# Final states of a state-space mixer as fp32r products in three terms

## The chip, the cores and the metric

The kernel runs on one core of a Trainium2 chip. The metric is the device time of one execution in microseconds (us); of several runs the median counts. The engines are called TensorE (PE), VectorE (DVE), ScalarE (ACT), GpSimd (POOL) and SyncE (SP). Each works through its own instructions in order. SP and POOL issue the transfers (DMAs) that this document speaks of.

## The reference, cut to what matters

One layer of a hybrid encoder works on 256 prompt tokens and 32 sample tokens with the same weights. A projection feeds a pooling mixer and a Mamba-2 mixer (SSD) with 32 heads of 64 features and a state of 128. Their outputs go through w_out, a norm and a residual; a feed-forward part (up projection, short convolution, gate, down projection) follows. The change concerns the final state of each head, which is an output beside the token outputs. In one line for a token group, with the tokens' l, the head's feature p and the state index n:

```
h_last[p, n] = sum_l  B[l, n] * decay[l] * dt[l] * x[l, p]   (+ elast * h0[p, n] for the sample)
```

For the prompt the sum runs over 256 tokens and the old state is zero; for the sample it runs over 32 tokens. B is shared by the 16 heads of a group; decay is the decay from token l to the last token.

## The kernel before, in words

The tokens lie on the free axis: 288 columns, 256 of the prompt and 32 of the sample. Features lie on the 128 partitions. All large products are fp32r products in three terms: a value is split into a high part (an fp32r copy by ACT) and a low part (the difference, by DVE), and PE adds high x high, high x low and low x high (`mm3`, L134 to L137). Weights come in by SP (`fetch_w`, L111), four raw buffers deep, and are split in pieces of 1024 columns (`split_w`, L117) into four buffers each for high and low.

`project` (L139) runs one group of 256 output features: per stage of its `ksplit` it fetches the weights, calls a hook (`before`) for the next stage, splits, multiplies, and at the end calls `done` for each accumulator. The instruction order on each engine comes from a scheduler that simulates the program; `keep_in_program_order` pins an instruction to its place on its engine, `issue_after` and `high_priority` steer it.

The work around the change, in order:
- The decay factors (L401 to L416): `dec` is decay times dt on 32 partitions (heads); PE transposes it into `tokd`, token rows of 128 x 32 per block of tokens. The sample's block is the last 128 tokens, with zeros in `tokd` (a memset on POOL) ahead of the 32 sample rows.
- B and x go through DRAM (`b_d`, `xs_d`) to become token rows. `btok` (L586, loaded by SP at L684 and L685) holds B with tokens on partitions: two prompt blocks and the sample's.
- `mix` holds the mixer's outputs as split pairs: 8 tiles of the pooling mixer (`mixp`) and 16 tiles of the SSD mixer (`mixs`, in the 16 slots of `apool`).
- The w_out groups (L740): group pairs 0 and 1 together, then 2 to 7 one by one, each over stages of k 8 to 15 (`mixs` 0 to 7), 16 to 23 (`mixs` 8 to 15) and 0 to 7 (`mixp`). `mix_out` (L668) squares each result into `msum` (ACT, then an addition on POOL) and stores it scaled by the norm's gain (`mg`, list `x1`). The last two squares go to `msq`.
- The states are four parts j of 512 columns (8 heads). `state_in` (L688) loads x rows and old state through POOL's queue, two buffers deep, and scales both on DVE. `state_p` (L706) multiplies two fp32 128x512 products for the prompt, copies the result (ACT) and stores it. `state_s` (L716) multiplies one fp32 product for the sample, copies it (ACT) and adds the old state. Parts 0 and 1 stand behind groups 2 and 3, with that addition on POOL. Parts 3 and 2 are loaded behind groups 4 and 5, and their products are pinned behind the last group and behind the products that finish `p_m` (the mean square, L737 and L758); their additions come on DVE in the line of the up projection (L804).
- The seam: `root(rm, p_m)` is a square root on ACT and a reciprocal on DVE (L235). `residual(t)` (L780) is a product and a sum on DVE; `in_line` (L773) keeps DVE's order. For each of 16 tiles k, ACT makes the high part of `hn` (L791), DVE the low part, ACT a square for the next norm, and PE multiplies seven accumulators (L815 to L820).
- The PSUM pool `acc_ps` has five banks, used in turn; `aux_ps` has three. `bpool` has 20 slots.

Of the kernel before, what the change touches and what calls it, by code (L numbers as in the profile page):

```python
# [8 lines left out]
F32 = mybir.dt.float32  # L9
F32R = mybir.dt.float32r  # L10
AF = mybir.ActivationFunctionType
ALU = mybir.AluOpType
# [4 lines left out]
P = 128  # L17
TC = {"schedule_with_timeline_sim": True}
D_MODEL = 2048
NP_ = 256  # L20
NS = 32
NT = NP_ + NS
# [3 lines left out]
HEADS = 32  # L26
D_FF = 5632
EPS = 1e-6
KD = D_MODEL // P
# [14 lines left out]
def body(  # L44
# [25 lines left out]
    act, dve, pool, pe, sp = nc.scalar, nc.vector, nc.gpsimd, nc.tensor, nc.sync  # L70
# [97 lines left out]
    def blocks_out(d, t, src, pool_):  # L168
# [17 lines left out]
        out=tri, in_=tri, pattern=[[1, P]], compare_op=ALU.is_ge, fill=0.0, base=0, channel_multiplier=-1  # L186
# [30 lines left out]
    start = ExitStack()  # L217
# [199 lines left out]

    bc = []
    for i in range(4):
# [166 lines left out]
    btok = op_.tile([P, 2, 3, P], F32, name="btok")  # L586
# [76 lines left out]
    wov = w_out  # L663
# [15 lines left out]
        x1.append(o)  # L679


    for gi in range(2):
        c = slice(gi * P, (gi + 1) * P)
        sp.dma_start(out=btok[:, gi, 0:2, :], in_=b_d[:NP_, c].rearrange("(b p) c -> p b c", p=P))  # L684
        sp.dma_start(out=btok[:, gi, 2, :], in_=b_d[NT - P :, c])  # L685
    stp = []

    def state_in(j):  # L688

        if not stp:  # L690
            poolp.close()
            stp.append(outp.enter_context(tc.tile_pool(name="stp", bufs=1)))
        x = stp[0].tile([P, 3, 512], F32, tag="sx", bufs=2, name="sx")
        h = stp[0].tile([P, 512], F32, tag="sh", bufs=2, name="sh")
        c = slice(512 * j, 512 * j + 512)
        pool.dma_start(out=x[:, 0:2, :], in_=xs_d[:NP_, c].rearrange("(b p) c -> p b c", p=P))
        pool.dma_start(out=x[:, 2, :], in_=xs_d[NT - P :, c])
        pool.dma_start(out=h, in_=state_ssd[:, c])
        x4 = x.rearrange("p b (r q) -> p b r q", r=8)
        w = tokd[:, :, 8 * j : 8 * j + 8].unsqueeze(3).broadcast_to([P, 3, 8, 64])  # L700
        dve.tensor_tensor(x4, x4, w, op=ALU.mult)
        h3 = h.rearrange("p (r q) -> p r q", r=8)
        dve.tensor_tensor(h3, h3, elast[:, 8 * j : 8 * j + 8].unsqueeze(2).broadcast_to([P, 8, 64]), op=ALU.mult)
        return x, h

    def state_p(j, x, h, pin=False):  # L706
        st = acc_ps.tile([P, 512], F32, tag="acc", name="pst")
        for b in range(2):
            ins = pe.matmul(st, btok[:, j // 2, b, :], x[:, b, :], start=b == 0, stop=b == 1)  # L709
            if pin:  # L710
                tc.keep_in_program_order(ins)
        ho = stp[0].tile([P, 512], F32, tag="ho", bufs=2, name="ho")
        act.activation(ho, st, AF.Copy)
        sp.dma_start(out=new_ssd_p[:, 512 * j : 512 * j + 512], in_=ho)

    def state_s(j, x, h, pin=False):  # L716
        st = acc_ps.tile([P, 512], F32, tag="acc", name="psts")
        ins = pe.matmul(st, btok[:, j // 2, 2, :], x[:, 2, :], start=True, stop=True)  # L718
        if pin:
            tc.keep_in_program_order(ins)  # L720
        act.activation(x[:, 2, :], st, AF.Copy)

        def add(eng=pool):
            ins = eng.tensor_tensor(h, h, x[:, 2, :], op=ALU.add)
            sp.dma_start(out=new_ssd_s[:, 512 * j : 512 * j + 512], in_=h)
            return ins

        return add

    late_in = {}  # L730

    def mix_before(g):
        def hook(kb, n):
            if g == 0 and kb == 0:
                pool_group(0)
            if g == 7 and kb == 0:
                pe.matmul(p_m, mean, msum, start=True, stop=False)  # L737
        return hook

    for grp in ((0, 1), (2,), (3,), (4,), (5,), (6,), (7,)):  # L740
        project(
            wov, [(256 * c, 256) for c in grp], mix, [(8, 8), (16, 8), (0, 8)],
            mix_before(grp[0]), lambda m, p_: mix_out(p_),
        )
        if 2 <= grp[0] < 4:
            x_h = state_in(grp[0] - 2)
            state_p(grp[0] - 2, *x_h)
            state_s(grp[0] - 2, *x_h)()
        elif 4 <= grp[0] < 6:
            late_in[grp[0] - 2] = state_in(grp[0] - 2)  # L750
        if grp[0] == 0:
            sp.dma_start(out=xT, in_=x_in)
            act.dma_start(out=new_sconv, in_=sc_stage)
            act.dma_start(out=new_pool, in_=np_stage)


    for i in range(2):
        tc.keep_in_program_order(pe.matmul(p_m, mean, last_sq[i], start=False, stop=i == 1))  # L758
# [14 lines left out]
    def in_line(f, *args, **kw):  # L773
        with ExitStack() as order:
            if line:
                order.enter_context(tc.issue_after(line[-1].ins))
            line.append(f(*args, **kw))
        return line[-1]

    def residual(t):  # L780
        in_line(dve.tensor_tensor, x1[t], x1[t], rm, op=ALU.mult)
        in_line(dve.tensor_tensor, x1[t], x1[t], xT[:, t, :], op=ALU.add)

    residual(0)
    for k in range(KD):
        if k % 2 == 0:
            raw = wpool.tile([P, 2, 896], F32, tag="raw", name="raw")
            with tc.high_priority(offset=ahead[0]):
                sp.dma_start(out=raw, in_=w_up1[:, k : k + 2, :])
        a = atile("hn")  # L790
        hi = act.activation(a[:, 0, :], x1[k], AF.Copy, scale=g_ffn_pre[:, k : k + 1])  # L791
# [369 lines left out]
```

## Time and profile before

| what | us |
|---|---|
| median of three runs (lowest, highest) | 1323.76 (1323.6, 1324.56) |
| the profiled execution | 1324.25 |
| its span (first to last instruction) | 1322.5 |
| PE busy in the span | 1314.3 (99%) |
| DVE busy | 882.4 (67%) |
| ACT busy | 667.3 (50%) |
| POOL busy | 222.4 (17%) |

Times in the rows of the profile are us from the span's start unless marked ns. The chain of work is followed back from the last instruction; each row is a start, a length, an engine and a line. PE's products overlap: the distance of two starts is what one costs, and it is shorter than the duration printed for it. A product in fp32 leaves two records, one in fp32r leaves one. "x4" counts records. In rows of the form "min/median/max" durations are in ns, landings of DMAs in us. The rows of stretches (windows) give the stretch, its length, then busy us of PE, PE's weight loads, DVE, ACT and POOL with their instruction counts, PE's granted clock, the DMA share and GB/s.

### The profile page before, as it was taken

The numbers are of one execution on the slowest core, as the hardware profiler recorded it, in microseconds if no ns is written. First come the engines' busy times: TensorE is split into PE (matmuls) and PEld (weight loads), VectorE is DVE, ScalarE is ACT, GpSimd is POOL, SyncE is SP. The second block draws the span as 40 slices with busy tenths as digits, with TensorE's granted clock in tenths as the row PEclk, the third lists the DMA queues.
The fourth block names the chain that finished last, engine by engine and source line by source line (L and its number), as shares of the span: only waits on it lengthen the run. The fifth ranks groups of instructions, "written<-read, shape, count | busy, mean of one in ns | idle before, by whom it ended". The sixth has DMA issues, their size and how long they took to land.

```text
span 1322.5 us, 25126 instructions
## 1 busy us (share of the span) xinstructions
PE 1314.3 (99%) x10063; PEld 1298.2 (98%) x10063; DVE 882.4 (67%) x1461; ACT 667.3 (50%) x1004; POOL 222.4 (17%) x351
## 2 busy tenths in 40 slices
PE   9999999999999999999999999999999999999998
PEld 9999999999999989999999999999999999999997
DVE  7899997779644379976766643345666666664544
ACT  7558876446443455654444443334444444444443
POOL 7221411211221100211211100001111111101110
PEclk9999999999999999999999999999999999999999
DMA  8668974465666446666454454455544544466653
GB/s 322 204 209 263 291 229 144 159 237 203 226 204 207 149 142 206 199 188 180 166 184 159 152 176 160 163 180 172 179 160 160 178 173 160 163 236 189 201 176 108
DMA packets 104021, 249.82 MB, mean 189 GB/s; under 512 B 63760, under 2 KB 69456, under 8 KB 81504
## 3 DMA queue, kind: packets, MB, share of 16 engines
q1 hardware_dynamic: 101984, 243.11, 56.1%
q0 software_dynamic: 1488, 4.92, 1.1%
q8 instruction: 79, 1.29, 0.4%
q14 instruction: 38, 0.31, 0.1%
q10 hardware_dynamic: 432, 0.19, 0.1%
HBM read 236.23 MB, written 11.95 MB: 188 GB/s over the span
## 4 chain that ended last, share of the span: by engine, by line
PE 99%; DMA 1%; ACT 0%; SPq 0%; issue 0%; DVE 0%
PE acc L135 31%; PE acc L137 31%; PE acc L136 31%; PE acc_x L137 1%; PE acc_x L135 1%; PE py L475 1%; PE acc_x L136 1%; DMA raw<-in_w_first 1%; PE pst L709 1%; PE run_a L1033 0%; PE low L1031 0%; PE run_b L1046 0%; PE py L477 0%; PE psts L718 0%; PE pdt L297 0%; PE py L481 0%
## 5 line engine op out<-in xcount | busy, mean ns | idle before, releaser
L130 DVE TENSOR_TENSOR wlo<-raw,whi 128x1024 fp32r<-128x1024 f32 (+1 forms) x386 | 463.0, 1200 | 340.8 <-ACT whi L129 338.5
L129 ACT ACTIVATE whi<-raw 128x1024 fp32r<-128x1024 f32 (+1 forms) x386 | 400.5, 1038 | 491.1 <-PE acc L136 394.9
L135 PE MATMUL acc<-hn,whi 128*128 128x288 f32 x1360 | 395.6, 295 | 0.0
L136 PE MATMUL acc<-hn,whi 128*128 128x288 f32 x1360 | 394.3, 293 | 0.0
L137 PE MATMUL acc<-hn,wlo 128*128 128x288 f32 x1360 | 393.2, 293 | 0.0
L135 PEld LDWEIGHTS acc<-hn,whi 128*128 128x128 f32 x1360 | 254.3, 188 | 0.5 <-ACT xsum L799 0.2
L136 PEld LDWEIGHTS acc<-hn,whi 128*128 128x128 f32 x1360 | 253.9, 188 | 0.1
L137 PEld LDWEIGHTS acc<-hn,wlo 128*128 128x128 f32 x1360 | 253.7, 188 | 0.0
L135 PE MATMUL acc<-xn,whi 128*128 128x288 f32 x688 | 203.1, 297 | 1.1 <-ACT whi L276 1.1
L136 PE MATMUL acc<-xn,whi 128*128 128x288 f32 x688 | 200.2, 293 | 0.0
L137 PE MATMUL acc<-xn,wlo 128*128 128x288 f32 x688 | 195.0, 295 | 0.0
L135 PE MATMUL acc<-fa,whi 128*128 128x288 f32 x660 | 194.2, 294 | 0.0
L136 PE MATMUL acc<-fa,whi 128*128 128x288 f32 x660 | 193.6, 293 | 0.0
L137 PE MATMUL acc<-fa,wlo 128*128 128x288 f32 x660 | 193.2, 293 | 0.0
L135 PEld LDWEIGHTS acc<-xn,whi 128*128 128x128 f32 x688 | 129.7, 189 | 2.8 <-ACT whi L276 1.4
L136 PEld LDWEIGHTS acc<-xn,whi 128*128 128x128 f32 x688 | 129.5, 188 | 0.2
L137 PEld LDWEIGHTS acc<-xn,wlo 128*128 128x128 f32 x688 | 126.5, 188 | 0.0
L135 PEld LDWEIGHTS acc<-fa,whi 128*128 128x128 f32 x660 | 124.2, 188 | 0.0
L137 PEld LDWEIGHTS acc<-fa,wlo 128*128 128x128 f32 x660 | 123.9, 188 | 0.0
L136 PEld LDWEIGHTS acc<-fa,whi 128*128 128x128 f32 x660 | 123.9, 188 | 0.0
L844 POOL COPY fc_stage<-ebuf 128x4 f32<-128x4 f32 x88 | 28.5, 324 | 526.4 <-DVE ebuf L843 455.5
L850 DVE SCALAR_TENSOR_TENSOR fc<-ebuf,pf,fc 128x290 f32<-128x290 f32 x176 | 90.0, 517 | 2.9 <-ACT fc L848 0.3
(286 smaller groups left out, 1701.6 us busy)
## 6 DMA issues: line engine op xcount, KB each, us to landing
raw<-in_w_up SPq DMA_DIRECT2D x80, 1024.0 KB, 4.8
raw<-in_w_in SPq DMA_DIRECT2D x38, 1024.0 KB, 5.1
raw<-in_w_down SPq DMA_DIRECT2D x32, 1024.0 KB, 4.8
raw<-in_w_out SPq DMA_DIRECT2D x24, 1024.0 KB, 4.8
raw<-in_w_down SPq DMA_DIRECT2D x16, 768.0 KB, 4.4
raw<-in_w_up SPq DMA_DIRECT2D x8, 896.0 KB, 4.5
gb<-g_d SPq DMA_DIRECT2D x8, 832.0 KB, 6.0
raw<-in_w_first SPq DMA_DIRECT2D x7, 768.0 KB, 9.0
```

The lines of the kernel that those rows point to most:

```text
L129: act.activation(hi, raw[:, k : k + n, :], AF.Copy)
L130: dve.tensor_tensor(lo, raw[:, k : k + n, :], hi.bitcast(F32), op=ALU.subtract)
L135: pe.matmul(out, wh, a[:, 0, :], start=start, stop=False)
L136: pe.matmul(out, wh, a[:, 1, :], start=False, stop=False)
L137: pe.matmul(out, wl, a[:, 0, :], start=False, stop=stop)
L475: pe.matmul(y[:, 0:256], xw[:, 0, c], m[:, j, 0:256], start=True, stop=False)
L709: ins = pe.matmul(st, btok[:, j // 2, b, :], x[:, b, :], start=b == 0, stop=b == 1)
L844: pool.tensor_copy(fc_stage[:, :, :, i], e[:, 256:324].rearrange("p (s c) -> p s c", c=34)[:, :, 0:2])
L850: dve.scalar_tensor_tensor(c, e[:, r_ : r_ + 290], pf[:, r_, i : i + 1], c, op0=ALU.mult, op1=ALU.add)
```

## The change

The final states are computed by fp32r products in three terms. B is split once into `bhi` and `blo`; each part's scaled x rows into `hi` and `lo`. A prompt part takes six 128x512 products. For the sample, the 32 token rows are put four times on the partitions (`token_rows`, four DMAs of 32 rows): the quarters hold low or high parts of B and of x such that one 128-row product sums all four terms. `tokd` gets the sample's factors four times as well (`dec_s`).

Part 0 stays behind group 2. Parts 3, 2 and 1 go behind the last group: the three sample products are pinned ahead of the last `p_m` products, the prompt products behind them. The buffers for x, old state and splits become single; part 2's split and all of part 1 live in slots of `apool` (those of the `mixs` tiles, the "tokens") and of `bpool`. Part 1's rows are loaded by POOL when group 7's hook asks for them, into the slots of `mixs` 5 to 7. Old-state additions read PSUM on DVE: those of parts 3 and 2 ahead of the `p_m` products in the program, part 1's in line behind `residual(0)`. In the first tile of the up projection the low part now precedes `residual(1)`. B rows come by POOL's queue, no longer by SP. The last stage of group 7 is split in two.

```diff
@@ decay factors
-    pool.memset(tokd[:, 2, :], 0.0)
+    dec_s = mp.tile([HEADS, 4, NS], F32, name="dec_s")
+    dve.tensor_copy(dec_s, dec[:, NP_:].unsqueeze(1).broadcast_to([HEADS, 4, NS]))
+    dec_s = dec_s.rearrange("h r s -> h (r s)")
...
-        pe.transpose(p_[:, 2, :], dec[:, o : o + P], id32)
+        pe.transpose(p_[:, 2, :], dec_s if b == 2 else dec[:, o : o + P], id32)
...
-        r_ = slice(P - NS, P) if b == 2 else slice(0, P)
-        dve.tensor_copy(tokd[r_, b, :], p_[r_, 2, :])
+        dve.tensor_copy(tokd[:, b, :], p_[:, 2, :])
@@ states
+    top, odd = slice(0, 2 * NS), (slice(0, NS), slice(2 * NS, 3 * NS))
+
+    def token_rows(eng, tile, src, c):
+        if isinstance(tile, list):
+            for b in range(2):
+                eng.dma_start(out=tile[b], in_=src[P * b : P * (b + 1), c])
+            last_ = tile[2]
+        else:
+            eng.dma_start(out=tile[:, 0:2, :], in_=src[:NP_, c].rearrange("(b p) c -> p b c", p=P))
+            last_ = tile[:, 2, :]
+        for r in range(4):
+            eng.dma_start(out=last_[NS * r : NS * (r + 1), :], in_=src[NP_:, c])
+
+    def sx_tile():
+        return stp[0].tile([P, 3, 512], F32, tag="sx", name="sx")
+
+    def state_pool():
...
+        blo = sp_.tile([P, 2, 2, P], F32R, name="blo")
...
+        token_rows(pool, b, b_d, slice(0, 2 * P))
...
+        for gi in range(2):
+            act.activation(bhi[:, gi], b[:, :, gi, :], AF.Copy)
+            dve.tensor_tensor(blo[:, gi], b[:, 0:2, gi, :], bhi[:, gi, 0:2, :].bitcast(F32), op=ALU.subtract)
+            for q in odd:
+                dve.tensor_tensor(
+                    bhi[q, gi, 2, :], b[q, 2, gi, :], bhi[q, gi, 2, :].bitcast(F32), op=ALU.subtract
+                )
+
+    def state_slot():
+        return atile("st").rearrange("p a t -> p (a t)")[:, :512]
+
+    def state_load(j, apart=False):
...
+        x = [state_slot().bitcast(F32) for _ in range(3)] if apart else sx_tile()
+        token_rows(pool, x, xs_d, slice(512 * j, 512 * j + 512))
+        if apart:
+            for b in (2, 0, 1):
+                x4 = x[b].rearrange("p (r q) -> p r q", r=8)
+                dve.tensor_tensor(x4, x4, w[:, b], op=ALU.mult)
+            return x
...
+    def state_in(x, apart=False):
+
+        if apart:
+            room = [state_slot() for _ in range(5)]
+            hi, lo = (room[3], room[4], room[0]), room[1:3]
+        else:
+            hi = stp[0].tile([P, 3, 512], F32R, tag="shi", name="shi")
+            lo = stp[0].tile([P, 2, 512], F32R, tag="slo", name="slo")
+        if apart:
+            for b in (2, 0, 1):
+                act.activation(hi[b], x[b], AF.Copy)
+                q = top if b == 2 else slice(0, P)
+                o = hi[2] if b == 2 else lo[b]
+                dve.tensor_tensor(o[q], x[b][q], hi[b][q].bitcast(F32), op=ALU.subtract)
...
-        for b in range(2):
-            ins = pe.matmul(st, btok[:, j // 2, b, :], x[:, b, :], start=b == 0, stop=b == 1)
+        terms = [(bw, b, y[b]) for b in range(2) for bw, y in ((bhi, hi), (bhi, lo), (stp[1], hi))]
+        for i, (bw, b, y) in enumerate(terms):
+            ins = pe.matmul(st, bw[:, j // 2, b, :], y, start=i == 0, stop=i == 5)
...
-        ins = pe.matmul(st, btok[:, j // 2, 2, :], x[:, 2, :], start=True, stop=True)
+        ins = pe.matmul(st, bhi[:, j // 2, 2, :], hi[2], start=True, stop=True)
...
-        act.activation(x[:, 2, :], st, AF.Copy)
...
+        def add(step=lambda f, *a, **k: f(*a, **k)):
+            n = 512 // len(h)
+            for i, t in enumerate(h):
+                step(dve.tensor_tensor, t, t, st[:, n * i : n * (i + 1)], op=ALU.add)
+                sp.dma_start(out=new_ssd_s[:, 512 * j + n * i : 512 * j + n * (i + 1)], in_=t)
@@ hook and groups of w_out
             if g == 7 and kb == 0:
+                late_in[2] = state_in(late_x[2], True)
+                late_x[1] = state_load(1, True)
+            if g == 7 and kb == 4:
+                late_in[1] = state_in(late_x[1], True)
...
-            wov, [(256 * c, 256) for c in grp], mix, [(8, 8), (16, 8), (0, 8)],
+            wov, [(256 * c, 256) for c in grp], mix,
+            [(8, 8), (16, 8)] + ([(0, 4), (4, 4)] if grp[0] == 7 else [(0, 8)]),
...
+        if grp[0] == 2:
...
+        elif grp[0] == 4:
+            late_in[3] = state_in(state_load(3))
+            late_h[3] = state_old(3)
+        elif grp[0] == 5:
+            late_x[2] = state_load(2)
+            late_h[2] = state_old(2, True)
+            late_h[1] = state_old(1, True)
@@ behind the mixer
+    late = (3, 2, 1)
+    add = {}
+    for j in late:
+        add[j] = state_s(j, late_in[j][0], late_h[j], pin=True)
+    for j in late[:2]:
+        add[j]()
     for i in range(2):
         tc.keep_in_program_order(pe.matmul(p_m, mean, last_sq[i], start=False, stop=i == 1))
-    late_add = []
-    for j in (3, 2):
-        state_p(j, *late_in[j], pin=True)
-        late_add.append(state_s(j, *late_in[j], pin=True))
+    for i, j in enumerate(late):
+        state_p(j, *late_in[j], late_x[2][i], pin=True)
...
     residual(0)
+    add[1](in_line)
     for k in range(KD):
...
-        if k + 1 < KD:
+        if 0 < k < KD - 1:
             residual(k + 1)
...
         if k == 0:
+            residual(1)
             act.activation(xsum, x1[k], AF.Square)
...
-        if 3 < k < 6:
-            in_line(late_add[k - 4], dve)
```

More of the change, by code (lines that the diff above doesn't have):

```diff
@@ L585, in body @@
     msum = op_.tile([P, NT], F32, name="msum")
-    btok = op_.tile([P, 2, 3, P], F32, name="btok")
+    bhi = op_.tile([P, 2, 3, P], F32R, name="bhi")
     msq = [op_.tile([P, NT], F32, name=f"msq{m}") for m in range(2)]
@@ L679, in mix_out @@
         x1.append(o)
[L682 to L685, printed above, removed]
     stp = []
-    def state_in(j):
-        if not stp:
[L691 to L698, printed above, removed]
+    top, odd = slice(0, 2 * NS), (slice(0, NS), slice(2 * NS, 3 * NS))
@@ new lines, in state_pool @@
+    def state_pool():
+        poolp.close()
+        sp_ = outp.enter_context(tc.tile_pool(name="stp", bufs=1))
+        blo = sp_.tile([P, 2, 2, P], F32R, name="blo")
+        stp.extend((sp_, blo))
+        b = sx_tile()[:, :, : 2 * P]
+        token_rows(pool, b, b_d, slice(0, 2 * P))
+        b = b.rearrange("p t (g n) -> p t g n", g=2)
+        for gi in range(2):
[5 more added lines that the diff above has]
+                )
@@ new lines, in state_slot @@
+    def state_slot():
+        return atile("st").rearrange("p a t -> p (a t)")[:, :512]
+    def state_load(j, apart=False):
+        if not stp:
+            state_pool()
+        w = tokd[:, :, 8 * j : 8 * j + 8].unsqueeze(3).broadcast_to([P, 3, 8, 64])
+        x = [state_slot().bitcast(F32) for _ in range(3)] if apart else sx_tile()
[5 more added lines that the diff above has]
+            return x
@@ L699, in state_in, with state_old @@
         x4 = x.rearrange("p b (r q) -> p b r q", r=8)
-        w = tokd[:, :, 8 * j : 8 * j + 8].unsqueeze(3).broadcast_to([P, 3, 8, 64])
         dve.tensor_tensor(x4, x4, w, op=ALU.mult)
[L702 to L706, printed above, removed]
+        return x if j != 2 else [x[:, b, :] for b in range(3)]
+    def state_old(j, apart=False):
+        if apart:
+            h = [btile("sh")[:, :256] for _ in range(2)]
+        else:
+            h = [stp[0].tile([P, 512], F32, tag="sh", name="sh")]
+        n = 512 // len(h)
+        for i, t in enumerate(h):
+            pool.dma_start(out=t, in_=state_ssd[:, 512 * j + n * i : 512 * j + n * (i + 1)])
+            w = elast[:, 8 * j + n // 64 * i : 8 * j + n // 64 * (i + 1)]
+            t3 = t.rearrange("p (r q) -> p r q", q=64)
+            dve.tensor_tensor(t3, t3, w.unsqueeze(2).broadcast_to([P, n // 64, 64]), op=ALU.mult)
+        return h
@@ new lines, in state_in @@
+    def state_in(x, apart=False):
+        if apart:
+            room = [state_slot() for _ in range(5)]
+            hi, lo = (room[3], room[4], room[0]), room[1:3]
+        else:
+            hi = stp[0].tile([P, 3, 512], F32R, tag="shi", name="shi")
+            lo = stp[0].tile([P, 2, 512], F32R, tag="slo", name="slo")
+        if apart:
+            for b in (2, 0, 1):
[3 more added lines that the diff above has]
+                dve.tensor_tensor(o[q], x[b][q], hi[b][q].bitcast(F32), op=ALU.subtract)
+        else:
+            act.activation(hi, x, AF.Copy)
+            dve.tensor_tensor(hi[top, 2, :], x[top, 2, :], hi[top, 2, :].bitcast(F32), op=ALU.subtract)
+            dve.tensor_tensor(lo, x[:, 0:2, :], hi[:, 0:2, :].bitcast(F32), op=ALU.subtract)
+            hi, lo = ([t[:, b, :] for b in range(t.shape[1])] for t in (hi, lo))
+        return hi, lo
@@ L713, in state_p, with state_s @@
         act.activation(ho, st, AF.Copy)
         sp.dma_start(out=new_ssd_p[:, 512 * j : 512 * j + 512], in_=ho)
-    def state_s(j, x, h, pin=False):
+    def state_s(j, hi, h, pin=False):
         st = acc_ps.tile([P, 512], F32, tag="acc", name="psts")
-        ins = pe.matmul(st, btok[:, j // 2, 2, :], x[:, 2, :], start=True, stop=True)
+        ins = pe.matmul(st, bhi[:, j // 2, 2, :], hi[2], start=True, stop=True)
         if pin:
             tc.keep_in_program_order(ins)
[L721 to L726, printed above, removed]
+        def add(step=lambda f, *a, **k: f(*a, **k)):
+            n = 512 // len(h)
+            for i, t in enumerate(h):
+                step(dve.tensor_tensor, t, t, st[:, n * i : n * (i + 1)], op=ALU.add)
+                sp.dma_start(out=new_ssd_s[:, 512 * j + n * i : 512 * j + n * (i + 1)], in_=t)
@@ L736, in hook @@
             if g == 7 and kb == 0:
+                late_in[2] = state_in(late_x[2], True)
+                late_x[1] = state_load(1, True)
+            if g == 7 and kb == 4:
+                late_in[1] = state_in(late_x[1], True)
+            if g == 7 and kb == 0:
                 pe.matmul(p_m, mean, msum, start=True, stop=False)
@@ L741, in body @@
         project(
-            wov, [(256 * c, 256) for c in grp], mix, [(8, 8), (16, 8), (0, 8)],
+            wov, [(256 * c, 256) for c in grp], mix,
+            [(8, 8), (16, 8)] + ([(0, 4), (4, 4)] if grp[0] == 7 else [(0, 8)]),
             mix_before(grp[0]), lambda m, p_: mix_out(p_),
         )
[L745 to L750, printed above, removed]
+        if grp[0] == 2:
+            j = grp[0] // 2 - 1
+            x = state_load(j)
+            hi, lo = state_in(x)
+            h = state_old(j)
+            state_p(j, hi, lo, x[:, 0, :])
+            state_s(j, hi, h)()
+        elif grp[0] == 4:
[5 more added lines that the diff above has]
+            late_h[1] = state_old(1, True)
         if grp[0] == 0:
```

4 lines of the change are left out of this document (2 added, 2 removed).

## The prediction, made before the changed kernel ran

> **What bounds the kernel now.** I read the page first, then the waits of TensorE, then the chain that ended last.
>
> ```profile
> span 1322.5 us, 25126 instructions
> ...
> PE 1314.3 (99%) x10063; PEld 1298.2 (98%) x10063; DVE 882.4 (67%) x1461; ACT 667.3 (50%) x1004; POOL 222.4 (17%) x351
> ...
> PE 99%; DMA 1%; ACT 0%; SPq 0%; issue 0%; DVE 0%
> ```
>
> ```profile
> PE idle L249 <- POOL mean L182: 1.2, 1, 1.2
> PE acc L135 <- ACT whi L276: 1.1, 1, 1.1
> PE y_ps L1076 <- ACT diag L1075: 0.6, 1, 0.6
> ```
>
> TensorE (PE) holds 99% of the chain, and its list of waits has only three entries, all at the two ends of the program. So a microsecond taken from PE's stream is a microsecond of the span, as long as no new wait appears, and a microsecond of VectorE (DVE), ScalarE (ACT) or GpSimd (POOL) costs nothing until PE waits for it. What counts is how long PE needs for the state products, and whether the work around them is ready when PE gets there. The chain in order of time shows the products and the seam between the mixer and the feed-forward part (start, us, what):
>
> ```profile
> 372.60 1.72 PE pst L709 x4
> 374.32 0.86 PE psts L718 x2
> 394.06 1.72 PE pst L709 x4
> ...
> 459.57 0.48 PE psum_m L737 x2
> 472.65 0.48 PE psum_m L758 x2
> 473.15 0.75 PE psum_m L758 x2
> 473.90 1.72 PE pst L709 x4
> 475.62 0.86 PE psts L718 x2
> 476.48 1.72 PE pst L709 x4
> 478.19 0.86 PE psts L718 x2
> 479.05 0.40 PE acc L135 x3
> ```
>
> Each of the four parts takes 1.72 + 0.86 = 2.58 us of PE. An fp32 product leaves two records: four records of pst are two products, so 128x512 in fp32 costs 0.86 us. All four parts: 10.32 us. The second product into psum_m at 473.15 takes 0.75 us where the other two take 0.48: about 0.27 us there is a wait for the last square.
>
> **The change on PE, part by part.** A part gets six fp32r products for the prompt and one for the sample, 7 in place of 3, all 128x512. No fp32r product of 512 columns is in this trace. The nearest are those of 288 and 320 columns at the end of the kernel, with the chain for their spacing:
>
> ```profile
> L1033 PE MATMUL run_a<-fa,whi 128*128 128x320 f32 x32 | 5.3, 309 | 0.0
> L1031 PE MATMUL low<-fa,wlo 128*128 128x288 f32 x32 | 5.2, 299 | 0.0
> ```
>
> ```profile
> 1300.88 1.06 PE low L1031 x8
> 1301.94 1.17 PE run_a L1033 x8
> ```
>
> One of 288 columns takes 1.06 / 8 = 0.1325 us, one of 320 columns 1.17 / 8 = 0.146 us: 0.46 ns a column in both. So 512 columns should take 0.234 us. Bounds: half an fp32 record of the same width, 0.43 / 2 = 0.215 us, from below; a whole fp32 record, 0.43 us, from above. I take 0.234, since two rows give the same rate. The page FP8 and Floating Point Precision of the Trainium skill (section TensorE Precision Notes) counts four passes for true fp32; if a product of reduced precision is one pass, an fp32r product is a quarter of 0.86 us, 0.215 us, and the 28 products come to 6.0 us instead of 6.6.
>
> Step by step:
> - Part 0, still behind group 2 of w_out: 2.58 becomes 7 x 0.234 = 1.64, a gain of 0.94 us.
> - Part 1 leaves its place at 394.06: a gain of 2.58 us there.
> - The seam, from the end of the last mixer product (472.65) to the first product of the up projection (479.05), is 6.40 us now. Afterwards it holds three sample products (0.70), the two psum_m products (0.96, with the wait for the square covered by the 0.70 ahead of it) and 18 prompt products (4.21): 5.87 us, a gain of 0.53.
>
> Sum: 4.05 us if PE waits nowhere.
>
> **The cover at the seam.** The state products there hide a chain on other engines: root of psum_m, reciprocal, first residual, first hn. It reads as follows on ACT and DVE (start, us, engine, line, what):
>
> ```profile
> 472.69 0.41 ACT L676 ACTIVATE msq<-acc 128x288 f32<-128x288 f32 x1 [0.77 <-PE acc L137]
> ...
> 473.94 0.50 ACT L236 ACTIVATE rm<-psum_m,eps_t 128x288 f32<-128x288 f32 x1 [0.45 <-PE psum_m L758]
> ...
> 477.45 0.53 ACT L791 ACTIVATE hn<-mg,par 128x288 fp32r<-128x288 f32 x1 [0.34 <-DVE mg L777]
> ```
>
> ```profile
> 474.48 1.95 DVE L237 RECIPROCAL rm<-rm 128x288 f32<-128x288 f32 x1 [2.99 <-ACT rm L236]
> 476.46 0.46 DVE L777 TENSOR_TENSOR mg<-mg,rm 128x288 f32<-128x288 f32 x1
> 476.95 0.46 DVE L777 TENSOR_TENSOR mg<-mg,xT 128x288 f32<-128x288 f32 x1
> 477.33 0.45 DVE L777 TENSOR_TENSOR mg<-mg,rm 128x288 f32<-128x288 f32 x1
> ...
> 478.19 0.52 DVE L777 SCALAR_TENSOR_TENSOR hn<-mg,par,hn 128x288 fp32r<-128x288 f32 x1
> ```
>
> psum_m ends at 473.90, the high half of hn ends at 477.98 (4.08 us later), the low half at 478.71 (4.81 later). PE has 5.15 us of state products after psum_m, so the high half is there 1.07 us early. Afterwards the cover is 4.21 us: the high half is early by only 0.13 us. The low half is needed after the seven products that read the high half (7 x 0.1325 = 0.93), at 5.14 against 4.81.
>
> New on this chain are the additions of the sample's state on DVE, which read PSUM. Their prices, by the addition that DVE does now and by a DVE operation of 256 columns out of PSUM:
>
> ```profile
> L724 DVE TENSOR_TENSOR sh<-sh,sx x2: 682/684/686, 487.3 to 490.5; 128x512 f32<-128x512 f32 x2
> ```
>
> ```profile
> 101.31 0.42 DVE L334 TENSOR_TENSOR ebuf<-acc,rstd 128x256 f32<-128x256 f32 x1
> ```
>
> Parts 3 and 2 (0.68 + 2 x 0.42 = 1.52 us) can start when the first sample product is done, about 473.1, and end about 474.6; the root then ends at 474.31 + 0.04 + 0.50 = 474.85. So they fit ahead of the reciprocal if DVE has nothing else left. Part 1 (two halves, 0.84) stands in line between the first residual and the low half; residual(1), two operations, moves behind the low half, so these exchange places at no cost. But the PSUM bank of part 1's sample product is wanted by the up projection's second accumulator (five banks in turn), about when that addition ends: 477.41 + 0.84 = 478.25, which is 4.35 us after psum_m, against 4.21 + 0.13 = 4.34. Three margins of 0.0 to 0.3 us are too thin to count on. I take 0.35 us of waiting (estimate; bounds 0 and one more addition of 0.68 with its hop, about 0.8). In exchange the two additions of 0.68 us leave the line of the up projection, where they stood at 487.3 and 490.5.
>
> **The loads and the preparation.** POOL issues 32 DMAs instead of 12, and the 4 on SP for btok go. What one costs and when it lands:
>
> ```profile
> 377.48 0.73 POOL L696 DMA_DIRECT2D sx<-xs_d  x1 [0.30 <-POOL sh L724]
> 378.21 0.55 POOL L697 DMA_DIRECT2D sx<-xs_d  x1
> ...
> 452.36 0.81 POOL L500 TENSOR_TENSOR msum<-msum,sq 128x288 f32<-128x288 f32 x1 [15.07 <-ACT sq L499]
> 454.68 1.49 POOL L500 TENSOR_TENSOR msum<-msum,sq 128x288 f32<-128x288 f32 x1 [1.51 <-ACT sq L499]
> ```
>
> ```profile
> L701 DVE TENSOR_TENSOR sx<-sx,tokd x4: 1758/1759/1761, 341.5 to 406.0; 128x1536 f32<-128x1536 f32 x4
> L721 ACT ACTIVATE sx<-psts x4: 585/599/601, 375.2 to 479.5; 128x512 f32<-128x512 f32 x4
> ...
> DMA to landing us min/median/max: 6.1/6.2/8.9
> ```
>
> Parts 0 and 3, and b, have time. The first load goes out when the pooling tiles are free, and it was at work on DVE at 341.5; part 0's products stand at 372.6. In these 31 us two loads now follow each other in one buffer: b, its split, x, its scaling (1.76), its copy (at most 3 x 0.60) and its differences (at most 3 x 0.68). That is 2 x 8.9 + about 8 = 26 us at the worst landing. POOL's only other work there is the sum of squares, once in 19 us. Part 2's scaled rows are in hand before the last group; its split needs the slots of the first five tokens' tiles only.
>
> Part 1 is the tight one. Its three slots are those of tiles 5 to 7, free when the first third of the last w_out group is done: the psum_m product at 459.57 marks that place. With six issues of 0.55 to 0.73 us the last sample piece is issued at about 459.6 + 2.95 = 462.5 and lands at 468.6 (6.1) to 471.4 (8.9). Then scale (0.68), copy (0.60) and difference (0.68), 1.96 us, give 470.6 to 473.4. PE wants it as third sample product at 472.65 + 0.47 = 473.1, ahead of psum_m. So the margin is +2.5 at the median and -0.3 at the worst landing. DVE and ACT have room, if not much:
>
> ```profile
> 460.00:466.00 6.00, 6.00 (x48) 6.00 (x47) 2.32 (x2) 1.49 (x2) 0.00 (x0) 1.00 0.46 153
> 466.00:472.50 6.50, 6.50 (x52) 6.50 (x51) 2.19 (x2) 2.71 (x4) 0.00 (x0) 1.00 0.44 141
> ```
>
> DVE is busy 4.5 of 12.5 us (fourth number), ACT 4.2 (fifth). Added are nine DVE operations of 128x512 (6.2 us) and six copies (3.6 us). POOL has nothing queued behind its DMAs there: the last sum of squares is at 454.68.
>
> The page SBUF — State Buffer of the Trainium skill (the "DVE blocks DMA" trap) says that a DVE operation in a two-port mode keeps GpSimd from writing descriptors, a rule against 20 more DMAs on POOL. Its own list leaves tensor_tensor out of these modes, and the DVE work of this stretch is of that kind; by it no term changes, and the issue rows above (0.55 to 0.73) show no such hold.
>
> The rest counts nothing: dec_s is one small DVE copy in place of a narrower copy and a memset (below the 0.42 us of the 128x256 row), and PE shows no wait at the transposes behind it; the split of the last stage of w_out in two is one more DMA issue with the same products.
>
> **Sum.** 4.05 - 0.35 = 3.7 us less. The profiled execution took 1324.25 us (span 1322.5, 1.75 around it), so 1320.55 by it; that execution stands 0.49 above the median of the runs, 1323.76, from which I forecast **1320.1 us**.
>
> **Rivals.**
> - *Thin seam, 0.22.* Part 1 lands at the late end, and DVE still has its scalings and differences in front of the additions and the reciprocal. PE waits up to 0.3 us for the third sample product, and up to four operations of 0.68 (2.7 us) delay the reciprocal. A third of that or all of it: 1.0 to 3.0 us back, 1321.1 to 1323.1, near 1322.0. For it: the margins above. Against: the median landing.
> - *The slots come late, 0.08; slower.* In order on POOL, the six DMAs of part 1 wait for the slots; if these come only with the end of the second third of the group (459.57 + 48 x 0.1325 = 465.9), the last piece lands at 465.9 + 2.95 + 6.1 = 475.0 and is ready at 476.9. PE stands 3.8 us at the pinned sample product, and the reciprocal comes 2.7 us later still: 6.5 back, 1326.6. It is slower by more than 0.2% where the first issue is later than about 465.7. Against it: the tiles 0 to 7 are read only in the first third.
> - *No gain at 512 columns, 0.04.* If an fp32r product of this width takes a whole fp32 record, 28 x 0.43 = 12.0 us stand against 10.3: 1325.5. Against it: two widths at one rate.
>
> **How the numbers follow.** The forecast has 0.66. A measurement of this kernel tells about 0.2%, 2.65 us, from no change: faster is below 1321.1, slower above 1326.4. Faster: 0.66 (forecast). Same: 0.22 + 0.04 = 0.26. Slower: 0.08. The range starts at 1319.0 (28 products at 0.215 are 0.53 us less, no wait gives 0.35, and a little for the spread of the runs) and reaches to 1323.8, over the thin seam with as much spread; the last two rivals are left out.
>
> **What would show it.** In the chain, the six products of pst of a part at about 1.40 us and psts at 0.23; nothing of pst between 380 and the seam but part 0's; the seam at about 6.2 us from the last mixer product to the first of up. Among PE's waits, nothing over 0.5 us at pst, psts, psum_m or acc. Issue of part 1's load about 13 us ahead of the last mixer product. What would make it wrong: a wait of PE at psts on DVE, a reciprocal that starts over 1 us behind the root, or PE waits at the ptok transposes.

## The result and the profile after

The changed kernel takes 1320.3 us (median of ten runs, 1319.83 to 1321.14), the one before 1323.68 in the same session: a ratio of 0.9976 (95% interval 0.9969 to 0.9984), 2.1 to 4.1 us less. The forecast was 1320.1. The profiled execution took 1319.88.

The page of the changed kernel and its waits of TensorE (us in total, times, longest) look as before: PE is the time, and there is no new entry among the waits.

```profile
span 1317.9 us, 25200 instructions
...
PE 1310.9 (99%) x10067; PEld 1298.6 (99%) x10067; DVE 894.7 (68%) x1486; ACT 670.9 (51%) x1010; POOL 232.6 (18%) x368
```

```profile
PE idle L249 <- POOL mean L182: 1.2, 1, 1.2
PE acc L135 <- ACT whi L276: 0.7, 1, 0.7
PE y_ps L1157 <- ACT diag L1156: 0.6, 1, 0.6
```

The chain of the changed kernel in order of time answers to the rows shown of before (start, us, what):

```profile
45.35 2.08 PE pdt L297 x32
...
372.54 1.40 PE pst L773 x6
373.94 0.23 PE psts L781
...
456.00 0.48 PE psum_m L805 x2
...
469.08 0.69 PE psts L781 x3
469.77 0.97 PE psum_m L841 x4
470.74 4.21 PE pst L773 x18
474.95 0.59 PE acc L135 x3
...
517.78 0.49 PE psum_t L905 x2
```

The same two outer marks in the chain of the kernel before:

```profile
46.00 2.08 PE pdt L297 x32
...
521.61 0.49 PE psum_t L824 x2
```

The two spans differ by 4.6 us, more than the medians. Part of that lies at the ends: pdt, which follows the first weights, came 0.65 us earlier in this execution (the first weights' transfer stands for 7.15 us in the chain, 7.81 before), and 0.77 us lie behind psum_t. Between pdt and psum_t PE alone sets the time, so that the difference of these two marks is a finer measure than a run's time: 475.61 us before, 472.43 after, 3.18 less. It repeats within 0.01 us where the order of the products is the same (472.43, and 472.42 twice below), and it is given for each experiment.

These 3.18 us split as follows:
- Part 0: 1.40 + 0.23 = 1.63 us where 2.58 stood; part 1's 2.58 us are gone from group 3. From pst (372.54, before 372.60) to the single psum_m product (456.00, before 459.57) the gain is 3.51 us.
- The seam from the end of the last mixer product to the first up product: 5.87 us (469.08 to 474.95) instead of 6.40, 0.53 gained.
- Given back ahead of the states: pdt to pst takes 327.19 us instead of 326.60, 0.59 lost.
- Given back behind the seam: the first up product to psum_t takes 42.83 us instead of 42.56, 0.27 lost; 0.19 of it is in the first row of up (0.59 for three products, before 0.40). What the other 0.08 are stays open.

That is 3.51 + 0.53 - 0.59 - 0.27 = 3.18.

**The 0.59 us** come from the order on PE. The chain around the transposes of the decay factors and the products into py, before:

```profile
104.90 0.30 PE ptok L413 x3
105.20 0.33 PE acc L136
...
128.83 0.58 PE py L475 x4
...
129.65 0.52 PE py L475 x4
```

and after:

```profile
104.25 0.24 PE ptok L415 x2
104.48 0.33 PE acc L136
...
106.67 0.17 PE ptok L415
106.84 0.33 PE acc L136
...
126.25 0.58 PE py L476 x4
...
127.26 0.33 PE acc L136
131.41 0.58 PE py L476 x4
```

Products that use only a part of the array (32 rows in ptok, 64 columns in py) stand in groups between full ones. The full product behind such a group takes 0.33 us instead of 0.13, and the first ptok takes 0.17 where the next ones take 0.06. Before, three ptok stand together, and two sets of py follow each other without a full product between them. After, dec_s comes one DVE copy later, the scheduler puts its transpose by itself, and two sets of py come apart: 13 such groups in the chain where 11 stood before. No wait shows it, since nothing is waited for. The page TensorEngine Tiling (Array Packing) of the Trainium skill (Key Properties) says that a change of the tiling mode drains TensorE. The rows fit that, with about 0.3 us for a group, but no row shows a drain itself.

### The profile page after: what moved, and what is told of

The parts are those of the page before. It is cut to its first block, busy times and chain, and to the rows that moved or that the text cites. A ratio compares the mean times of both kernels' runs of the same rounds, so it can differ in the third digit from the quotient of the medians.

```text
span 1317.9 us, 25200 instructions
## 1 busy us (share of the span) xinstructions
PE 1310.9 (99%) x10067; PEld 1298.6 (99%) x10067; DVE 894.7 (68%) x1486; ACT 670.9 (51%) x1010; POOL 232.6 (18%) x368
## 4 chain that ended last, share of the span: by engine, by line
PE 99%; DMA 1%; ACT 0%; SPq 0%; issue 0%; DVE 0%
PE acc L135 31%; PE acc L137 31%; PE acc L136 31%; PE py L476 1%; PE acc_x L135 1%; PE acc_x L137 1%; PE acc_x L136 1%; DMA raw<-in_w_first 1%; PE pst L773 0%; PE run_a L1114 0%; PE low L1112 0%; PE run_b L1127 0%; PE py L478 0%; PE pdt L297 0%; PE py L482 0%; PE py L480 0%
## 5 line engine op out<-in xcount | busy, mean ns | idle before, releaser
L921 POOL COPY ebuf<-pf 128x2 f32<-128x2 f32 x88 | 75.5, 858 | 129.5 <-DVE fc L931 83.0
```

The lines of the kernel that those rows point to most:

```text
L921: pool.tensor_copy(e[:, 258:260], pf[:, 4:6, i])
```

## The experiments

All are edits of the changed kernel (1320.3 us, 472.43 us from pdt to psum_t). Ratios are to the kernel before, with their intervals.

| kernel | median us | ratio to before | pdt to psum_t |
|---|---|---|---|
| fp32_products | 1324.54 | 1.0002 (0.9993 to 1.0011) | 475.97 |
| part1_back | 1322.18 | 0.9987 (0.9978 to 0.9995) | 473.95 |
| dec_early | 1319.96 | 0.9969 (0.9958 to 0.9981) | 471.84 |
| tidy | 1319.33 | 0.9965 (0.9953 to 0.9978) | 471.84 |
| late_slots | 1320.23 | 0.9976 (0.9967 to 0.9986) | 472.42 |
| sums_first | 1321.93 | 0.9991 (0.9982 to 1.0000) | 473.90 |
| sample_thrice | 1321.81 | 0.9987 (0.9977 to 0.9996) | 474.31 |
| after_again | 1320.82 | 0.9981 (0.9972 to 0.9989) | 472.42 |
| one_behind | 1319.42 | 0.9970 (0.9957 to 0.9982) | 471.66 |
| late_touch | 1324.12 | 1.0004 (0.9995 to 1.0013) | 476.04 |

Most of the intervals overlap with that of the changed kernel. Differences between the versions are therefore read from the marks, each from one profiled execution.

**fp32_products.** The arithmetic alone undone.

```diff
-        terms = [(bw, b, y[b]) for b in range(2) for bw, y in ((bhi, hi), (bhi, lo), (stp[1], hi))]
-        for i, (bw, b, y) in enumerate(terms):
-            ins = pe.matmul(st, bw[:, j // 2, b, :], y, start=i == 0, stop=i == 5)
+        for b in range(2):
+            ins = pe.matmul(
+                st, bhi[:, j // 2, b, :].bitcast(F32), hi[b].bitcast(F32), start=b == 0, stop=b == 1
+            )
...
-        ins = pe.matmul(st, bhi[:, j // 2, 2, :], hi[2], start=True, stop=True)
+        ins = pe.matmul(st, bhi[:, j // 2, 2, :].bitcast(F32), hi[2].bitcast(F32), start=True, stop=True)
```

> The changed kernel with all its loads, splits and places, but the state products are fp32 again: two for the prompt and one for the sample per part, on the high parts alone (the low terms of the prompt are left out). Theory A, the gain is TensorE time of the products: part 0 goes back from 1.64 to 2.58 us, the three sample products from 0.69 to 2.58, the three prompt parts from 4.21 to 5.16, and the 0.19 us wait at the up projection's second product goes; 3.6 us more than the changed kernel (1320.3), so about 1323.9, where the kernel before is. Rival B, the gain comes from where the parts stand: no difference to 1320.3.

Its chain at the seam:

```profile
470.46 2.58 PE psts L782 x6
473.03 0.97 PE psum_m L842 x4
474.00 5.15 PE pst L772 x12
479.15 0.40 PE acc L135 x3
```

From pdt to psum_t it takes 3.54 us more than the changed kernel, and its time is that of the kernel before (1.0002). Theory A holds, B falls: with fp32 products the new places bring no net gain. Without the 0.59 us that it gives back ahead of the states, as the changed kernel does, it would stand 0.23 us under the kernel before by the marks; that is about the wait for the square (0.27), which the new order covers. The extra time at the first up products goes with the longer cover (0.40 again).

**part1_back.** The cover at the seam cut.

```diff
-        if grp[0] == 2:
-            j = grp[0] // 2 - 1
+        if 2 <= grp[0] < 4:
+            j = grp[0] - 2
...
-                late_x[1] = state_load(1, True)
-            if g == 7 and kb == 4:
-                late_in[1] = state_in(late_x[1], True)
...
-            late_h[1] = state_old(1, True)
...
-    late = (3, 2, 1)
+    late = (3, 2)
...
-    add[1](in_line)
```

> fp32r products as in the changed kernel, but part 1 stands behind group 3 again, so that only parts 3 and 2 lie at the seam. Theory A, the seam needs about 4.1 us of products behind psum_m as cover: twelve products give 2.81, so TensorE waits about 1.3 us for the first hn (a wait on ACT hn in its list), and the time is about 1.1 us over the changed kernel, 1321.4. Rival B, the cover is not needed because the low half or the weights can come in another order: within 0.2 us of 1320.3, and no wait.

Its waits of PE begin with the one that was expected, at its size:

```profile
PE acc L135 <- ACT hn L868: 1.3, 1, 1.3
```

It takes 1.52 us more from pdt to psum_t, against 1.1 expected; the first up row still holds extra time (0.67 us for three products), though the expectation had counted 0.2 us there as gone. Another 0.11 us lie between part 0's pst and psum_m, where 1.74 us were added and part 1's products are only 1.63; the rows show no cause for them. Theory A holds: the products of part 1 are worth more at the seam, where they stand over a wait, than behind group 3.

**dec_early and tidy.** The first puts the transposes together again; the second also moves part 1's addition.

```diff
-    dec = htile("dec", tag="gsum")
-    for (o, n), go, last in zip(BLK, (0, 256, 384), (255, 383, 415)):
-        act.activation(dec[:, o : o + n], g[:, go : go + n], AF.Exp, bias=g[:, last : last + 1], scale=-1.0)
-    dve.tensor_tensor(dec, dec, dt, op=ALU.mult)
+    dec = mp.tile([HEADS, NP_ + P], F32, name="dec")
+    dt4 = mp.tile([HEADS, NP_ + P], F32, name="dt4")
+    four = lambda t: t.unsqueeze(1).broadcast_to([HEADS, 4, NS])
+    rows4 = lambda t: t[:, NP_:].rearrange("h (r s) -> h r s", r=4)
+    dve.tensor_copy(dt4[:, :NP_], dt[:, :NP_])
+    dve.tensor_copy(rows4(dt4), four(dt[:, NP_:]))
+    for (o, n), go, last in zip(BLK[:2], (0, 256), (255, 383)):
+        act.activation(dec[:, o : o + n], g[:, go : go + n], AF.Exp, bias=g[:, last : last + 1], scale=-1.0)
+    act.activation(rows4(dec), four(g[:, 384:]), AF.Exp, bias=g[:, 415:416], scale=-1.0)
+    dve.tensor_tensor(dec, dec, dt4, op=ALU.mult)
...
-        pe.transpose(p_[:, 2, :], dec_s if b == 2 else dec[:, o : o + P], id32)
+        pe.transpose(p_[:, 2, :], dec[:, P * b : P * b + P], id32)
```

In tidy also:

```diff
-    for j in late[:2]:
+    for j in late:
         add[j]()
...
-    add[1](in_line)
```

> The changed kernel, with the sample's four-fold decay factors made in one tile with the prompt's, so that the three transposes of dec stand together again and the products into py run in eight groups instead of nine. Theory A, each group of products that use only a part of the array costs about 0.3 us around it (the first one 0.17 instead of 0.06, the next full product 0.33 instead of 0.13), and the changed kernel has two groups more than the one before: 0.6 us less, and 326.6 us from pdt to pst as in the kernel before, instead of 327.2. Rival B, the 0.6 us between these two marks is an accident of the execution: 327.2 again.

> dec_early together with the addition of part 1's state ahead of the psum_m products like those of parts 3 and 2, no longer in line behind the first residual. Theory A: the 0.19 us wait at the up projection's second product goes (its bank is free earlier), the reciprocal starts up to 0.2 us later; with the 0.6 us of dec_early the time is about 1319.5, 0.8 us under the changed kernel. Rival B, the later reciprocal takes it all back: 1319.7 with a wait at the first up product of 0.1 to 0.2 us.

The chain of dec_early:

```profile
45.70 2.08 PE pdt L297 x32
105.11 0.30 PE ptok L418 x3
...
128.67 0.58 PE py L479 x4
129.49 0.52 PE py L479 x4
...
372.31 1.40 PE pst L776 x6
```

pdt to pst is 326.61 us, as in the kernel before (326.60), though DVE makes two copies more than there. In the runs whose groups stand as in the changed kernel it is 327.19 or 327.20 each time, eight executions. In dec_early the chain holds 11 groups again. So the 0.59 us belong to the order, not to the execution, and theory A holds. (The median, 1319.96, is only 0.34 us lower, within the intervals.)

In tidy the wait at the first up row stayed: 0.59, and 471.84 us like dec_early. The reciprocal started no later against psum_m than in dec_early (0.57 us behind its end in both). So the bank of part 1's sample product, which the prediction held to be wanted too early, was not what the up product waited for. ACT's row of the first hn and the weight loads of the changed kernel (PEld, with the idle time ahead of the load and what ended it) point elsewhere:

```profile
474.29 0.54 ACT L873 ACTIVATE hn<-mg,par 128x288 fp32r<-128x288 f32 x1
```

```profile
474.32 0.19 PEld L773 LDWEIGHTS pst<-st,blo 128*128 128x128 f32 x1
474.87 0.43 PEld L135 LDWEIGHTS acc<-hn,whi 128*128 128x128 f32 x3 [0.36 <-ACT hn L873]
```

The load of the first up product began only when hn was there, though its weights had long been ready. hn came at 474.83, 0.12 us ahead of PE's mark in the chain (474.95), but the load takes 0.19 and was no longer hidden. That mark is the modelled end of the last pst. Start to start, the first up product came 0.32 us behind the last pst, and 0.24 in one_behind below. So a part of the 0.19 us can be the product's own wait for hn; the rows do not divide it between product and load.

**one_behind, with after_again beside it.** A test of that reading, on top of dec_early.

```diff
-    for j in late:
-        add[j] = state_s(j, late_in[j][0], late_h[j], pin=True)
     for j in late[:2]:
+        add[j] = state_s(j, late_in[j][0], late_h[j], pin=True)
         add[j]()
     for i in range(2):
         tc.keep_in_program_order(pe.matmul(p_m, mean, last_sq[i], start=False, stop=i == 1))
+    add[1] = state_s(1, late_in[1][0], late_h[1], pin=True)
```

> The changed kernel once more, as a mark for the two beside it. All theories: 0.9976 of the kernel before within its interval (about 1320.2), 327.2 us from pdt to pst, the first three up products 0.59 us.

> dec_early with part 1's sample product behind the two psum_m products instead of ahead of them. Theory C, the 0.19 us at the first up products is the weight load of the first one, which stands with its product behind the wait for the first hn and is no longer hidden, since hn comes only 0.1 us ahead of PE: psum_m now ends 0.23 us earlier against PE's stream, hn is 0.35 us early, and the first three up products take 0.40 us; 0.2 us less than dec_early from pdt to psum_t (471.65 against 471.84). Theory D, the wait is for a PSUM bank: 0.59 again.

The chain of one_behind:

```profile
468.62 0.46 PE psts L784 x2
469.09 0.97 PE psum_m L843 x4
470.06 0.23 PE psts L784
470.29 4.20 PE pst L776 x18
474.48 0.44 PE acc L135 x3
```

after_again gave its marks once more (327.19 us from pdt to pst, 0.59 in the first up row). In one_behind, where hn is earlier against PE, that row falls from 0.59 to 0.44 (0.40 expected), and pdt to psum_t from 471.84 to 471.66. Theory C holds in that the late hn is the cause, D falls. This version is the best one measured: 0.9970 of the kernel before, and by the marks 0.77 us under the changed kernel. The runs tell it from the kernel before, but their intervals overlap with those of the changed kernel.

**sums_first.** psum_m ahead of the sample products.

```diff
+    for i in range(2):
+        tc.keep_in_program_order(pe.matmul(p_m, mean, last_sq[i], start=False, stop=i == 1))
     for j in late:
         add[j] = state_s(j, late_in[j][0], late_h[j], pin=True)
     for j in late[:2]:
         add[j]()
-    for i in range(2):
-        tc.keep_in_program_order(pe.matmul(p_m, mean, last_sq[i], start=False, stop=i == 1))
```

> The changed kernel with the two psum_m products ahead of the three sample products. Theory A: the wait of 0.27 us for the last square is back (psum_m takes about 1.23 us instead of 0.97), the cover behind it grows to 4.9 us, and DVE's two additions now compete with the reciprocal, which may start up to 1.1 us behind the root: 0.1 to 0.6 us more than 1320.3. Rival B, the order does not matter: psum_m 0.97 and the seam 5.87 as in the changed kernel.

The waits of PE, and ACT's row of the first hn:

```profile
PE acc L135 <- ACT hn L873: 1.1, 1, 1.1
```

```profile
475.95 0.60 ACT L776 ACTIVATE sx<-pst 128x512 f32<-128x512 f32 x1 [0.74 <-PE pst L773]
476.44 0.53 ACT L873 ACTIVATE hn<-mg,par 128x288 fp32r<-128x288 f32 x1
```

It is 1.47 us slower from pdt to psum_t, more than the 0.1 to 0.6 expected. The wait for the square (0.27) and the later reciprocal (1.0 us behind the root) came as expected. Not foreseen was ACT: with the residual late, the scheduler's order put the copy of the last state product ahead of hn, and that copy waits for the last pst. The sample products ahead of psum_m thus keep DVE's additions out of the chain as well as covering the square.

**sample_thrice.**

```diff
-        ins = pe.matmul(st, bhi[:, j // 2, 2, :], hi[2], start=True, stop=True)
-        if pin:
-            tc.keep_in_program_order(ins)
+        for i in range(3):
+            ins = pe.matmul(st, bhi[:, j // 2, 2, :], hi[2], start=i == 0, stop=i == 2)
+            if pin:
+                tc.keep_in_program_order(ins)
```

> The changed kernel with each sample product issued three times (the sum is then three times too large), as it would be with three terms as products of their own instead of the rows four times on the partitions. Theory A, TensorE's stream is the time: eight products of 0.234 us more, 1.87 us, so about 1322.2. Rival B, the seam has room that hides the six of them that stand there: 0.47 us more, 1320.8.

1.88 us more from pdt to psum_t, where eight products of 0.234 are 1.87. Theory A holds, B falls: the rows four times on the partitions save these.

**late_slots and late_touch.** The load of part 1's rows made late. In late_slots other slots were set aside for part 1's split ahead of its load:

```diff
-            room = [state_slot() for _ in range(5)]
+            room = room or [state_slot() for _ in range(5)]
...
+                late_room.extend(state_slot() for _ in range(5))
                 late_x[1] = state_load(1, True)
...
-                late_in[1] = state_in(late_x[1], True)
+                late_in[1] = state_in(late_x[1], True, late_room)
```

> The changed kernel, but part 1's rows go into the slots of token tiles 10 to 12 instead of 5 to 7, so that the sample's rows can be loaded only when the second third of the last w_out group is done. Theory A, the margin of that load is about 2 us: the four sample pieces are issued from about 462.3 on instead of 456.6, land 5 to 6.4 us after their issue, at about 469.5, and are ready about 471.5 where TensorE wants them at 469.5; it waits about 2 us at the sample product, and the reciprocal comes up to 2.7 us later still: 1322.3 to 1325. Rival B, pieces of 32 rows land within 3 us: no wait over 0.3 us, 1320.3 to 1320.6.

The load went out at 455.45, as in the changed kernel (455.51): slots seem to be given out as tiles come into use, and the edit changed nothing. So this run decides nothing between the two theories. late_touch claims the five tiles first:

```diff
                 late_room.extend(state_slot() for _ in range(5))
+                for t in late_room:
+                    tc.keep_in_program_order(pool.memset(t.bitcast(F32)[:, :1], 0.0))
                 late_x[1] = state_load(1, True)
```

(with the load's DMAs pinned behind them).

> The changed kernel, with five slots claimed by one-column memsets on POOL ahead of part 1's load, so that its sample rows wait for a token tile of the second third of the last w_out group. Theory A, the load's margin is about 2 us: the sample pieces are issued from about 462.3 on instead of 456.6 and land 5 to 6.4 us after their issue, their scale, copy and difference end about 471.5, PE wants them at 469.5 and waits about 2 us at psts; the reciprocal, behind the remaining differences on DVE, comes up to 2.7 us later still: 1322.3 to 1325. Rival B, the pieces of 32 rows land within 3 us: no wait over 0.3 us, 1320.3 to 1320.6.

POOL's queue, DVE's work on part 1, and the waits of PE in late_touch:

```profile
462.61 1.99 POOL L695 DMA_DIRECT2D st<-xs_d  x4 [1.26 <-PE acc L137]
```

```profile
469.57 0.68 DVE L731 TENSOR_TENSOR st<-st,tokd 128x512 f32<-128x512 f32 x1
470.17 1.34 DVE L787 TENSOR_TENSOR sh<-sh,psts 128x512 f32<-128x512 f32 x3
471.43 0.68 DVE L763 TENSOR_TENSOR st<-st 64x512 fp32r<-64x512 f32 x1
```

```profile
PE psts L783 <- DVE st L763: 2.0, 1, 2.0
```

The wait of 2.0 us is that of theory A, B falls. But the way there was another: the pieces land 2.4 to 4.5 us after their issue here, and DVE, in order, put the additions of the other two parts (1.34 us) between part 1's scaling and its difference. The reciprocal was not delayed further (0.03 us behind the root). Still 3.61 us were lost from pdt to psum_t. Most of the rest is in the stretches behind the wait (length; PE, PEld, DVE, ACT, POOL; granted clock, the number before the DMA share):

```profile
473.00:474.00 1.00, 1.00 (x5) 0.74 (x5) 0.00 (x0) 0.26 (x1) 0.00 (x0) 0.82 0.20 66
474.00:475.00 1.00, 1.00 (x4) 0.81 (x3) 0.73 (x1) 0.24 (x1) 0.00 (x0) 0.50 0.00 0
475.00:476.00 1.00, 1.00 (x3) 0.71 (x3) 1.00 (x1) 0.00 (x0) 0.00 (x0) 0.50 0.03 8
476.00:477.00 1.00, 1.00 (x4) 0.80 (x3) 0.93 (x3) 0.60 (x1) 0.00 (x0) 0.50 0.00 0
477.00:478.00 1.00, 1.00 (x6) 0.83 (x5) 0.87 (x3) 0.00 (x0) 0.00 (x0) 0.97 0.29 113
```

The clock was granted at half for over 3 us, and the 18 products into pst took 5.74 us instead of 4.21, 1.53 us on top of the wait:

```profile
473.70 5.74 PE pst L775 x18
```

## Why the prediction was right, step by step

- *The price of a product of 512 columns*, 0.234 us from two narrower widths: 1.40 / 6 = 0.233. The two rows were the better guide than the 0.215 estimated from the pass count of the page FP8 and Floating Point Precision of the Trainium skill (TensorE Precision Notes).
- *Parts 0 and 1, and the seam*: 1.64 forecast, 1.63 found; 0.70, 0.96 and 4.21 forecast, 0.69, 0.97 and 4.21 found. The square is covered by the sample products, shown by sums_first, where its wait came back. fp32_products shows that without this arithmetic the change gains nothing on balance.
- *The cover*: hn was forecast 0.13 us ahead of PE and came 0.12 ahead, by the same mark of the chain. The prediction read this as early enough, though thin; it was not. part1_back shows what a shorter cover costs.
- *Waiting at the seam*, taken at 0.35: 0.27 found up to psum_t, of which 0.19 is in the first up row. The size held, partly by luck: of the three thin margins that the estimate covers, the bank, on which the prediction dwelt, cost nothing (tidy). The wait was at the high half of hn, which came too late for the first product and its weight load to be hidden (one_behind).
- *Part 1's load*: its first issue 13.6 us ahead of the end of the last mixer product (13 forecast), landing 5.0 to 6.4 us after the issue, its sample difference (466.07, 0.68 long) done 2.8 us before PE wanted it (2.5 forecast). The thin seam did not come. The rival of late slots is real: late_touch, where the sample rows are issued about 5 us later against PE's stream, is no faster than the kernel before. Its price came otherwise than the rival had it: no later reciprocal, but half the clock behind the wait.
- *"The rest counts nothing"* was wrong by 0.59 us. The step looked for a wait at the ptok transposes and counted the copy as small; what it missed is that a later operand changes the scheduler's order on PE, and that groups of partial products cost time around them (dec_early).

The two givebacks (0.59 + 0.27) against the 0.35 allowed make 0.5 us: the gain by the marks is 3.18 where 3.7 was forecast. The medians do not resolve that, and it is in part luck that the measured median lies as close as 0.2 us to the forecast.

## What to carry to other kernels

Where TensorE holds 99% of the chain, price a change in PE's own spacing (start to start), take a missing width from two measured ones, and then list what the old, slower products were hiding: the chain behind them, and the first product and weight load that need its result. Compare the order of PE's instructions before and after, not its waits alone: a small copy elsewhere moved two groups of products and cost a sixth of the gain. Keep pinned waits well inside their margin, since a wait can cost more than its length.

## What the runs showed of the hardware that was not expected

- A wait of PE of 2.0 us (late_touch) was followed, from about 1.4 us behind its end, by over 3 us at a granted clock of 0.50. After waits of 1.3 us (part1_back) and 1.1 us (sums_first) it stayed at 1.00. The page TensorE: Matmul & The Clock Gate of the Trainium skill (Why this matters for your kernels) warns of idle gaps over about 3 us; here the gap ahead of the slower clock was 2.0 us. This is one profiled execution; where between 1.3 and 2.0 us it begins, and whether it always does, no run shows.
- A group of products on a part of the array costs about 0.3 us around it: 0.59 us for two groups more (13 against 11), the same to 0.02 us in every profiled execution here.
- The weight load of the first up product began only when the product's other operand, hn, was there, although its weights had been ready for over 10 us. With hn 0.12 us ahead of the chain's mark for PE, the first three products took 0.19 us longer than before.
